# The causal mask of an attention head: from a TensorE product to an add inside VectorE's maximum pass

## The chip, the cores and the metric

The kernel runs on one core of a Trainium2 chip. A core has five engines with queues of their own: PE (TensorE: matrix products into PSUM; PEld is its weight load), DVE (VectorE), ACT (ScalarE), POOL (GpSimd) and SP, which here only issues DMAs. Each queue runs in the order in which the program was written out; engines wait for one another by semaphores. The metric is the device time of one execution in microseconds (us), lower is better.

## The reference

One decoder layer on 512 tokens of width 1024, in float32: a layer norm; an input projection; a gated linear attention branch in four heads; a latent attention branch in eight heads (MLA); gates, an output projection and a layer norm; a squared-ReLU MLP with hidden width 4096 and a last layer norm. The change is in the MLA heads, whose core is:

```
scale = MLA_QK ** -0.5                                  # MLA_QK = 192
for blk in range(seq // Q_BLOCK):                       # 4 blocks of 128 queries
    q0, q1 = blk * Q_BLOCK, (blk + 1) * Q_BLOCK
    s = (einsum('bhqd,bhkd->bhqk', q_nope[:, :, q0:q1], k_nope[:, :, :q1])
         + einsum('bhqr,bkr->bhqk', q_rope[:, :, q0:q1], k_rope[:, :q1])) * scale
    mask = (q0 + arange(Q_BLOCK))[:, None] >= arange(q1)[None, :]
    p = softmax(where(mask, s, -inf), axis=-1)
    outs.append(einsum('bhqk,bhkv->bhqv', p, v[:, :, :q1]))
```

So a block of 128 queries sees 128, 256, 384 or 512 keys, and only its last 128 columns need a mask: a triangle.

## The kernel before

Nearly every matrix product is made from split operands: a float32 array is rounded to a high part on ACT and its remainder, the low part, is made on DVE (`split`, and lines 180 and 181 in `pump` for the weights), and a product is then three products, high by high, high by low and low by high (lines 231 to 233, 264 to 266, 1134 to 1136). Weights come from HBM through a stream that is planned ahead: `pump` issues their DMAs on SP's queue (line 168) into three raw buffers, and splits them in turn.

Work that runs beside the big products is written as Python generators; `tick` steps each of them once after each weight block. The order on each engine is then set by the framework's scheduler, which reorders the whole program by its own estimate of time (`schedule_with_timeline_sim=True`), with a few `issue_after` gates. So an edit in one place can change the order of instructions in another place.

Start-up. Two of the four x tiles are loaded on SP's queue, then the first weights. DVE takes statistics of a tile in two halves (line 349), POOL takes the power of -0.5 (352), and the tile is normalised, on ACT for tile 0 (356, which waits for `nmr` of line 355) and on DVE for tile 1 (358). PE transposes them (367), ACT writes the high part `h` (370) and DVE the low part (374, 375). The first products (264 to 266) multiply them by the first weights, whose split is `xh` (180, ACT) and `xl` (181, DVE). Small constants are loaded on ACT's DMA queue: `cb` (line 395, a pack of gains, the 128x128 triangle `neg` and the frequencies `invf`), positions, level masks `lmi` and `wa`. `prep` turns them into what later stages need (413 to 421).

An MLA head (`mla_head`) goes through its four query blocks. For block i with n = 128(i+1) keys: five products into one PSUM bank (813 to 817); a sixth (818) adds the triangle by multiplying a bf16 identity with the bf16 triangle `negb` into the last 128 columns; DVE takes the negated row maximum `mx` from PSUM (820); ACT takes the exponential from PSUM with `mx` as bias, writes `Pm` to SBUF and sums the row (823); DVE inverts the sum and scales the row (824, 825). After the four blocks PE transposes the rows (837), they are split, and multiplied with the values. Heads are spawned in pairs, and run beside the projections of the next pair and of `w_o_gla` and `w_o_mla`. SBUF tiles come from pools: B has 22 buffers of 2 KB per partition, taken in turn.

The end. `ln2_stats` and `ln2` make the last layer norm, tile by tile, beside and behind the last products.

Of the kernel before, what the change touches and what calls it, by code (L numbers as in the profile page):

```python
# [10 lines left out]
F32 = mybir.dt.float32  # L11
F32R = mybir.dt.float32r
BF = mybir.dt.bfloat16
I32 = mybir.dt.int32
U8 = mybir.dt.uint8
AF = mybir.ActivationFunctionType
ALU = mybir.AluOpType
AX = mybir.AxisListType

P = 128  # L20
T = 512
# [27 lines left out]
PACK_B = 3 + 2 + NK + GH + 2 * NK + 2 * NK + P + 32  # L49
# [3 lines left out]
def tile_hybrid_block(ctx: ExitStack, tc: tile.TileContext, I, out, dbg=None):  # L53
    nc = tc.nc
    dbg = dbg or {}
    consts = ctx.enter_context(tc.tile_pool(name="consts", bufs=1))
# [8 lines left out]
    def nm(s):  # L65
        uid[0] += 1
        return f"{s}_{uid[0]}"
# [4 lines left out]
    def A(shape, dt=F32, n="a"):  # L72
        tag, bufs = ("C", 8) if n in TAG_C else (n, TAG_W[n]) if n in TAG_W else ("A", 24)
        return pa.tile(shape, dt, tag=tag, bufs=bufs, name=nm(n))

    def B(shape, dt=F32, n="b"):
        return pb.tile(shape, dt, tag="B", name=nm(n))

    def S(shape, dt=F32, n="s"):
        return sm.tile(shape, dt, tag=n, name=nm(n))  # L80
# [4 lines left out]
    def PX(shape=(P, T), dt=F32, n="px"):  # L85
        return px.tile(list(shape), dt, tag="px", name=nm(n))
# [4 lines left out]
    act = nc.scalar.activation  # L91
# [4 lines left out]
    mm = nc.tensor.matmul  # L96
# [7 lines left out]
    def split(src, hi, lo, scale=None):  # L104
        if scale is None:
            act(hi, src, AF.Copy)
            return vtt(lo, src, f(hi), op=ALU.subtract)
        else:
            act(hi, src, AF.Copy, scale=scale)
            return stt(lo, src, scale, f(hi), op0=ALU.mult, op1=ALU.subtract)  # L110
# [13 lines left out]
    ident = ca[:, 0:P]  # L124
# [2 lines left out]
    mhalf = consts.tile([P, 8], F32, name="mhalf")  # L127
    nc.vector.memset(mhalf, -0.5)
    identr = consts.tile([P, P], F32R, name="identr")
    identb = consts.tile([P, P], BF, name="identb")  # L130
    negb = consts.tile([P, P], BF, name="negb")


    stream = []
# [255 lines left out]


    act(identr, ident, AF.Copy)
    act(identb, ident, AF.Copy)
    cb = consts.tile([P, PACK_B], F32, name="cb")
    nc.scalar.dma_start(cb, I["c_pack_b"])
    cut = np.cumsum([0, 3, 2, NK, GH, 2 * NK, NK, NK, P, 32]).tolist()
    qag, kvg, glg, bga, bgt, ln1g, ln1b, neg, invf = [cb[:, cut[i]:cut[i + 1]] for i in range(9)]
    posi = consts.tile([P, NT], I32, name="posi")
    nc.scalar.dma_start(posi, I["positions"].rearrange("(t p) -> p t", p=P))
    lmask = consts.tile([P, len(LEVELS), 64], U8, name="lmask")  # L400
# [10 lines left out]
    def prep():  # L411
        with tc.issue_after(last_in.ins):
            vts(hbg, bgt, 0.5, None, op0=ALU.mult)
            nc.vector.tensor_copy(negb, neg)
            nc.vector.tensor_copy(lmask, lmi)
        posf = consts.tile([P, NT], F32, name="posf")
        with tc.issue_after(last_in.ins):
            nc.vector.tensor_copy(posf, posi)
        ang = B([P, NT, 32], F32, "ang")
        for tt in range(NT):  # L420
            vts(ang[:, tt, :], invf, posf[:, tt:tt + 1], None, op0=ALU.mult)
        yield
        angs = []
        for sh in (0.0, 0.25):
            kq = B([P, NT, 32], F32, "kq")
            vts(kq, ang, 1.0 / (2.0 * math.pi), sh, op0=ALU.mult, op1=ALU.add)
            vts(kq, kq, MAGIC, None, op0=ALU.add)
            vts(kq, kq, MAGIC, None, op0=ALU.subtract)
            r = B([P, NT, 32], F32, "rr")
            stt(r, kq, -TWO_PI_1, ang, op0=ALU.mult, op1=ALU.add)  # L430
            stt(r, kq, -TWO_PI_2, r, op0=ALU.mult, op1=ALU.add)
            stt(r, kq, -TWO_PI_3, r, op0=ALU.mult, op1=ALU.add)
            vts(r, r, sh * 2.0 * math.pi, PI_F, op0=ALU.add, op1=ALU.min)
            vts(r, r, -PI_F, None, op0=ALU.max)
            angs.append(r)
            yield
        act(sn2[:, :, 32:], angs[0], AF.Sin)
        act(cs2[:, :, :32], angs[1], AF.Sin)
        nc.vector.tensor_copy(cs2[:, :, 32:], cs2[:, :, :32])
        vts(sn2[:, :, :32], sn2[:, :, 32:], -1.0, None, op0=ALU.mult)  # L440
        yield
# [311 lines left out]
    scale = HQ ** -0.5  # L753
# [47 lines left out]
    def mla_head(h, hl, qn, kn, vt):  # L801
        for _ in range((0 if h == MH - 1 else STAG) * hl):
            yield
        KK, qs = KKs[0], QS[h]
        Ps = []
        P02 = B([P, T], F32, "P02")
        for i in range(NT):
            n = P * (i + 1)
            nn = max(n, 2 * P)
            c = slice(i * P, (i + 1) * P)  # L810
            p = PX()
            o = p[:, :nn]
            mm(o, qn[:, 0, c], kn[:, 0, :nn], start=True, stop=False)
            mm(o, qn[:, 0, c], kn[:, 1, :nn], start=False, stop=False)
            mm(o, qn[:, 1, c], kn[:, 0, :nn], start=False, stop=False)
            mm(o, qs[:, c], KK[:, 0, :nn], start=False, stop=False)
            mm(o, qs[:, c], KK[:, 1, :nn], start=False, stop=False)
            mm(p[:, c], identb, negb, start=False, stop=True)
            mx = S([P, 1], F32, "mx")
            nc.vector.tensor_reduce(mx, p[:, :n], axis=AX.X, op=ALU.max, negate=True)  # L820
            Pm = P02[:, :P] if i == 0 else P02[:, P:] if i == 2 else B([P, T], F32, "Pm")
            sme = S([P, 1], F32, "sme")
            act(Pm[:, :n], p[:, :n], AF.Exp, bias=mx, accum_out=sme)
            nc.vector.reciprocal(sme, sme)
            vts(Pm[:, :n], Pm[:, :n], sme, None, op0=ALU.mult)
            Ps.append(Pm)
            if i != 0:
                yield

        PT = [A([P, 2, T], F32R, "PT0"), A([P, 2, T], F32R, "PT1"), B([P, 2, 256], F32R, "PT2")]  # L830
        plan_t = ([(i, 0, i) for i in range(4)], [(i - 1, 1, i) for i in range(1, 4)] + [(3, 3, 3)],
                  [(i - 2, 2, i) for i in range(2, 4)])
        for b, (pl, pt) in enumerate(zip(plan_t, PT)):
            n = len(pl) * P
            p = PX()
            for cc, j, i in pl:
                nc.tensor.transpose(p[:, cc * P:(cc + 1) * P], Ps[i][:, j * P:(j + 1) * P], ident)  # L837
            split(p[:, :n], pt[:, 0, :], pt[:, 1, :])
            if b != 1:
                yield  # L840
        PT0, PT1, PT2 = PT
        while vt[NT - 1] is None:
            yield
        o = PX()
        for j in range(NT):
            c = slice(hl * P, (hl + 1) * P)
            vh, vl = vt[j][:, 0, c], vt[j][:, 1, c]
            if j == 0:
                ph, pl, od = PT0[:, 0, :], PT0[:, 1, :], o
            elif j == 1:  # L850
                ph, pl, od = PT1[:, 0, :384], PT1[:, 1, :384], o[:, 128:]
            elif j == 2:
                ph, pl, od = PT2[:, 0, :], PT2[:, 1, :], o[:, 256:]
            else:
                ph, pl, od = PT1[:, 0, 384:], PT1[:, 1, 384:], o[:, 384:]
            mm(od, vh, ph, start=j == 0, stop=False)
            mm(od, vh, pl, start=False, stop=False)
            mm(od, vl, ph, start=False, stop=j == NT - 1)
        yield
        om = A([P, 2, T], F32R, "omT")  # L860
        st["om"] = split(o, om[:, 0, :], om[:, 1, :])
        omT[h] = om
# [17 lines left out]
    for hf in range(2):  # L880
        if hf == 1:
            finish(t_ln1)
            t_prep = spawn(prep())
        for i in range(2):
            gemm_tm([PL["lat", i]], hT, half, ev_lat(i), tts=(2 * hf, 2 * hf + 1))
# [73 lines left out]
    t0, mv = mla_pair(0)  # L959
    mv()  # L960
    y_gla(1)
    t1, mv = mla_pair(1)
    mv(lambda: finish(*t0))
    t2, mv = mla_pair(2)
    mv(lambda: finish(*t1))
    t3, mv = mla_pair(3)
# [72 lines left out]
    LN2 = [None] * NT  # L1039

    def ln2_stats(tt, j, w=T, c0=0):
        if LN2[tt] is None:
            LN2[tt] = (S([P, 4 if tt == 3 else 2, 6], F32, f"bst{tt}"), S([P, 2], F32, "mv"))
        c = j * T + c0
        i = 2 * j + c0 // w if tt == 3 else j
        nc.vector.bn_stats(LN2[tt][0][:, i, :], res[tt][:, c:c + w])
# [69 lines left out]
    def win_f2(ci, hid):  # L1116
# [60 lines left out]
        for t in range(2):  # L1177
            with tc.issue_after(st["p6"].ins):
                ln2_stats(t, 0)
        for t in range(2):  # L1180
            o = tile_product((8, 9), t)
            vtt(res[t][:, T:], res[t][:, T:], o, op=ALU.add)
            ln2_stats(t, 1)
            ln2(t)
# [104 lines left out]
```

## Time and profile before

| | us |
|---|---|
| runs shown (3), median | 900.85 (900.52 to 900.86) |
| profiled execution, its own time | 900.46 |
| its span, first to last instruction | 898.7 |
| PE busy in the span | 878.0 |
| DVE busy | 570.2 |
| ACT busy | 432.7 |
| POOL busy | 172.8 |

The span is what the profile sees; 1.8 us of the execution's time lie around it. Where rows are shown, a timeline row is: start and length in us, engine, line, operation, output<-inputs, shape, count, and in brackets idle time before it and what ended that. A row by source line is: engine, operation, count, then the shortest, median and longest duration in ns, and the first and last start. A row by form gives busy us and mean ns after the bar. A row of windows is: the stretch, its length, then busy us (instructions) of PE, PEld, DVE, ACT and POOL, the granted PE clock, the share of DMA engines busy, and GB/s.

### The profile page before, as it was taken

How to read it: one execution, taken by the hardware profiler on the slowest of the kernel's cores; microseconds unless marked ns; L12 is line 12 of the kernel's file. 1: busy time of each engine (PE TensorE's matmuls, PEld its weight loads, DVE VectorE, ACT ScalarE, POOL GpSimd, SP SyncE). 2: the span in 40 equal slices, each digit the busy share in tenths (PEclk: the TensorE clock that was granted, in tenths of full speed). 3: DMA queues.
4: the chain of work that ended last, by engine and by line, in shares of the span. 5: the costliest groups of instructions: out<-in, count | busy, mean ns of one | idle time of the engine just before them, and what ended most of it. 6: DMA issues, size and time to landing. Idle time of an engine off the chain costs nothing.

```text
span 898.7 us, 11716 instructions
## 1 busy us (share of the span) xinstructions
PE 878.0 (98%) x4472; PEld 746.2 (83%) x4472; DVE 570.2 (63%) x927; ACT 432.7 (48%) x731; POOL 172.8 (19%) x201
## 2 busy tenths in 40 slices
PE   5999999999999999999999999999999999999995
PEld 5988888888888888888888888988888888888884
DVE  7835855575634243657765797998556656753687
ACT  5555443444444333435644424266457536644661
POOL 0003542443511010000000002103400520142022
PEclk9999999999999999999999999999999999999998
DMA  7413223212213332212206628004960991298075
GB/s 237 129 47 94 73 69 94 71 47 71 71 42 94 88 107 55 87 35 72 94 24 257 190 69 287 18 1 102 317 144 0 268 251 44 59 307 196 1 187 94
DMA packets 63048, 100.94 MB, mean 112 GB/s; under 512 B 7649, under 2 KB 31585, under 8 KB 62993
## 3 DMA queue, kind: packets, MB, share of 16 engines
q1 hardware_dynamic: 48256, 64.04, 23.2%
q0 software_dynamic: 12816, 32.51, 14.9%
q10 hardware_dynamic: 1920, 3.66, 1.2%
q8 instruction: 35, 0.57, 0.3%
q14 instruction: 21, 0.16, 0.1%
HBM read 82.36 MB, written 3.67 MB: 96 GB/s over the span
## 4 chain that ended last, share of the span: by engine, by line
PE 96%; ACT 1%; DVE 1%; POOL 1%; DMA 1%; issue 0%; POOLq 0%; SPq 0%; DVEq 0%; ACTq 0%
PE mm L231 16%; PE mm L233 15%; PE mm L232 15%; PE mm L264 6%; PE mm L266 6%; PE mm L265 6%; PE px L1134 3%; PE px L1135 3%; PE px L1136 3%; PE mm L1134 2%; PE mm L1135 2%; PE mm L1136 2%; PE px L680 2%; PE px L837 1%; PE px L266 1%; PE px L264 1%
## 5 line engine op out<-in xcount | busy, mean ns | idle before, releaser
L181 DVE TENSOR_TENSOR wlo<-wraw,whi 128x1024 fp32r<-128x1024 f32 (+1 forms) x104 | 117.7, 1133 | 164.4 <-ACT whi L180 157.1
L231 PE MATMUL mm<-h,whi 128*128 128x512 f32 x416 | 162.7, 392 | 0.4 <-ACT gt L924 0.4
L232 PE MATMUL mm<-h,whi 128*128 128x512 f32 x416 | 162.4, 390 | 0.0
L180 ACT ACTIVATE whi<-wraw 128x1024 fp32r<-128x1024 f32 (+1 forms) x104 | 100.3, 964 | 120.6 <-PE mm L232 69.8
L233 PE MATMUL mm<-h,wlo 128*128 128x512 f32 x416 | 154.9, 390 | 0.0
L1162 POOL DMA_DIRECT2D res<-ev x54 | 46.8, 978 | 240.1 <-ACT ev L1160 192.0
L231 PEld LDWEIGHTS mm<-h,whi 128*128 128x128 f32 x416 | 78.1, 188 | 16.4 <-ACT gt L924 0.6
L233 PEld LDWEIGHTS mm<-h,wlo 128*128 128x128 f32 x416 | 77.9, 188 | 16.3 <-DVE wlo L181 0.3
L232 PEld LDWEIGHTS mm<-h,whi 128*128 128x128 f32 x416 | 78.2, 188 | 15.6
L265 PE MATMUL mm<-wlo,h 128*128 128x512 f32 x128 | 50.3, 393 | 0.0
L266 PE MATMUL mm<-whi,h 128*128 128x512 f32 x128 | 50.2, 392 | 0.0
L264 PE MATMUL mm<-whi,h 128*128 128x512 f32 x128 | 49.7, 403 | 0.0
L1216 ACT ACTIVATE relu<-mm 128x512 f32<-128x512 f32 x32 | 18.8, 595 | 56.8 <-PE mm L233 56.8
L352 POOL TENSOR_TENSOR mv<-mv,mhalf 128x1 f32<-128x1 f32 x4 | 4.6, 1155 | 211.9 <-DVE mv L351 211.9
L619 POOL TENSOR_TENSOR rp<-rp 128x256 f32<-128x256 f32 x32 | 31.6, 986 | 60.3 <-ACT E L624 43.6
L626 DVE TENSOR_TENSOR M<-E,qk 128x512 f32<-128x512 f32 x32 | 26.9, 840 | 16.6 <-ACT E L624 16.6
L624 ACT ACTIVATE E<-rp 128x512 f32<-128x512 f32 x32 | 20.4, 638 | 27.7 <-POOL rp L620 27.7
L181 DVE TENSOR_TENSOR wlo<-wq,whi 128x1024 fp32r<-128x1024 f32 x15 | 18.3, 1223 | 19.7 <-ACT whi L180 19.7
L180 ACT ACTIVATE xh<-wraw 128x1024 fp32r<-128x1024 f32 (+1 forms) x20 | 18.7, 953 | 24.8 <-PE mm L266 15.8
L620 POOL TENSOR_TENSOR rp<-rp 128x256 f32<-128x256 f32 x32 | 28.5, 891 | 10.3 <-ACT q L649 8.1
L266 PEld LDWEIGHTS mm<-whi,h 128*128 128x128 f32 x128 | 24.1, 188 | 5.0
L265 PEld LDWEIGHTS mm<-wlo,h 128*128 128x128 f32 x128 | 24.1, 188 | 4.3
(374 smaller groups left out, 2237.7 us busy)
## 6 DMA issues: line engine op xcount, KB each, us to landing
wraw<-in_w_in_dram SPq DMA_DIRECT2D x40, 512.0 KB, 3.6
wraw<-in_w_ff_dram SPq DMA_DIRECT2D x32, 512.0 KB, 8.1
wq<-in_w_ff_dram POOLq DMA_DIRECT2D x32, 512.0 KB, 8.8
res<-ev POOLq DMA_DIRECT2D x54, 256.0 KB, 8.6
wraw<-in_w_o_gla_dram SPq DMA_DIRECT2D x8, 512.0 KB, 3.7
wraw<-in_w_o_mla_dram SPq DMA_DIRECT2D x8, 512.0 KB, 3.4
wraw<-in_w_out_dram SPq DMA_DIRECT2D x8, 512.0 KB, 4.4
wraw<-in_w_in_dram SPq DMA_DIRECT2D x8, 360.0 KB, 5.1
```

The source lines that it names most:

```text
L180: st["ins"] = act(hi[:, :nk, :n], raw[:, :nk, :n], AF.Copy)
L181: vtt(lo[:, :nk, :n], raw[:, :nk, :n], f(hi[:, :nk, :n]), op=ALU.subtract)
L231: mm(o, hi[:, c], xh, start=first, stop=False)
L232: mm(o, hi[:, c], xl, start=False, stop=False)
L233: mm(o, lo[:, c], xh, start=False, stop=last)
L264: mm(o, xh, hi[:, :n], start=opens, stop=False, skip_group_check=share)
L265: mm(o, xh, lo[:, :n], start=False, stop=False, skip_group_check=share)
L266: mm(o, xl, hi[:, :n], start=False, stop=last, skip_group_check=share)
L1134: mm(o, xh[:, c], hi[:, pp, cols], start=opens, stop=False, skip_group_check=True)
L1135: mm(o, xh[:, c], lo[:, pp, cols], start=False, stop=False, skip_group_check=True)
L1136: mm(o, xl[:, c], hi[:, pp, cols], start=False, stop=hf == 1 and pp == 1, skip_group_check=True)
L1162: nc.gpsimd.dma_start(res[tt + t][:, j * T:(j + 1) * T], e, accum_op=ALU.add)
```

## The change

The bf16 identity and triangle go, and with them the sixth product. A float32 mask `cmask` of 128x512 takes their place: zeros in its first 384 columns (written by POOL), the triangle in its last 128 (copied by DVE in `prep`). The maximum becomes one DVE instruction that adds the last n columns of `cmask` to the scores, multiplies by -1, writes that to `Pm` in SBUF, and folds the minimum of it into `mx`. In the built program each of these is two DVE instructions: the pass itself and a read of its accumulator into `mx` (128x1). The exponential then reads `Pm` from SBUF instead of the scores from PSUM, and writes in place, with scale -1.

To make room, the constant pack is loaded by two DMAs: `cb` keeps 49 columns, and the triangle and frequencies (160 columns) go to `cn`, a tile of pool B, whose DMA stands further back. The last layer norm's statistics tile moves to pool B.

```diff
-    identb = consts.tile([P, P], BF, name="identb")
-    negb = consts.tile([P, P], BF, name="negb")
+    cmask = consts.tile([P, T], F32, name="cmask")
...
-    act(identb, ident, AF.Copy)
-    cb = consts.tile([P, PACK_B], F32, name="cb")
-    nc.scalar.dma_start(cb, I["c_pack_b"])
+    nc.gpsimd.memset(cmask[:, :T - P], 0.0)
+    cb = consts.tile([P, PACK_B - P - 32], F32, name="cb")
+    nc.scalar.dma_start(cb, I["c_pack_b"][:, :PACK_B - P - 32])
+    cn = B([P, P + 32], F32, "cn")
+    nc.scalar.dma_start(cn, I["c_pack_b"][:, PACK_B - P - 32:])
...
-            nc.vector.tensor_copy(negb, neg)
+            nc.vector.tensor_copy(cmask[:, T - P:], neg)
...
-            mm(o, qs[:, c], KK[:, 1, :nn], start=False, stop=False)
-            mm(p[:, c], identb, negb, start=False, stop=True)
+            mm(o, qs[:, c], KK[:, 1, :nn], start=False, stop=True)
             mx = S([P, 1], F32, "mx")
-            nc.vector.tensor_reduce(mx, p[:, :n], axis=AX.X, op=ALU.max, negate=True)
             Pm = P02[:, :P] if i == 0 else P02[:, P:] if i == 2 else B([P, T], F32, "Pm")
+            nc.vector.tensor_tensor_reduce(Pm[:, :n], p[:, :n], cmask[:, T - n:], -1.0, 3.0e38,
+                                           op0=ALU.add, op1=ALU.min, accum_out=mx)
             sme = S([P, 1], F32, "sme")
-            act(Pm[:, :n], p[:, :n], AF.Exp, bias=mx, accum_out=sme)
+            act(Pm[:, :n], Pm[:, :n], AF.Exp, scale=-1.0, bias=mx, accum_out=sme)
...
-            LN2[tt] = (S([P, 4 if tt == 3 else 2, 6], F32, f"bst{tt}"), S([P, 2], F32, "mv"))
+            LN2[tt] = (B([P, 4 if tt == 3 else 2, 6], F32, "bst"), S([P, 2], F32, "mv"))
```

In the written-out order, 64 instructions leave PE (32 products with 32 weight loads), 32 come to DVE, one leaves ACT and one DMA joins its queue, one comes to POOL. SP's order is the same, and so is everything behind the first MLP block. In the start-up (about the first 40 us) and among the MLA heads the scheduler also put the remaining instructions in another order, and a few neighbours are swapped from there up to the first MLP block. In the start-up: on ACT the first `xh` split stands ahead of the normalisation of x tile 0 (before, behind it); on DVE both halves of tile 1's statistics stand ahead of `nmr` (before, one half); on ACT the fourth `xh` split stands after two evacuations `h` instead of after six `h` and two `lnt`; on DVE the statistics of tiles 2 and 3 both stand ahead of the split `xl` of the fifth weight block (before, those of tile 2 alone), and the copy into `cmask` stands ahead of the sixth.

More of the change, by code (lines that the diff above doesn't have):

```diff
@@ L392, in tile_hybrid_block @@
     act(identr, ident, AF.Copy)
-    act(identb, ident, AF.Copy)
-    cb = consts.tile([P, PACK_B], F32, name="cb")
-    nc.scalar.dma_start(cb, I["c_pack_b"])
+    nc.gpsimd.memset(cmask[:, :T - P], 0.0)
[3 more added lines that the diff above has]
+    nc.scalar.dma_start(cn, I["c_pack_b"][:, PACK_B - P - 32:])
     cut = np.cumsum([0, 3, 2, NK, GH, 2 * NK, NK, NK, P, 32]).tolist()
-    qag, kvg, glg, bga, bgt, ln1g, ln1b, neg, invf = [cb[:, cut[i]:cut[i + 1]] for i in range(9)]
+    qag, kvg, glg, bga, bgt, ln1g, ln1b = [cb[:, cut[i]:cut[i + 1]] for i in range(7)]
+    neg, invf = cn[:, :P], cn[:, P:]
     posi = consts.tile([P, NT], I32, name="posi")
```

## The prediction

> **What bounds the kernel now.** I read the page first, then the stretch of the MLA heads and a stretch of the start-up in the view of windows.
>
> ```profile
> span 898.7 us, 11716 instructions
> PE 878.0 (98%) x4472; PEld 746.2 (83%) x4472; DVE 570.2 (63%) x927; ACT 432.7 (48%) x731; POOL 172.8 (19%) x201
> PE 96%; ACT 1%; DVE 1%; POOL 1%; DMA 1%; issue 0%; POOLq 0%; SPq 0%; DVEq 0%; ACTq 0%
> ```
>
> PE is busy for 98% of the span and carries 96% of the chain that ended last: time taken off PE's queue is time gained, and a wait put on PE is time lost, almost anywhere.
>
> ```profile
> core 0: us, PE busy (x) PEld busy (x) DVE busy (x) ACT busy (x) POOL busy (x), PEclk, DMA share, GB/s
> 15.00:20.00 5.00, 5.00 (x31) 4.84 (x30) 4.91 (x14) 3.95 (x7) 0.00 (x0) 1.00 0.99 326
> 363.00:470.00 107.00, 107.00 (x622) 91.30 (x621) 71.04 (x170) 53.16 (x133) 0.00 (x0) 1.00 0.19 56
> ```
>
> Among the heads PE is never idle and DVE has 36 of 107 us free. In the start-up stretch DVE is as full as PE (4.91 of 5): there DVE's order matters.
>
> **The products removed.** The rows of line 818, then PE's queue around the first and the last of the 32:
>
> ```profile
> L818 PEld LDWEIGHTS <-identb x32: 94/96/99, 364.6 to 468.1; 128*128 128x128 bf16 x32
> L818 PE MATMUL px<-negb,identb x32: 220/230/233, 364.6 to 468.2; 128*128 128x128 bf16 x32
> ```
>
> ```profile
> 364.45 0.28 PE L817 MATMUL px<-KK,QS 128*128 128x256 f32 x1
> 364.57 0.23 PE L818 MATMUL px<-negb,identb 128*128 128x128 bf16 x1
> 364.61 0.36 PE L814 MATMUL px<-qn,qn 128*128 128x256 f32 x1
> 364.82 0.28 PE L815 MATMUL px<-qn,qn 128*128 128x256 f32 x1
> ...
> 467.92 0.39 PE L817 MATMUL px<-KK,QS 128*128 128x512 f32 x1
> 468.15 0.23 PE L818 MATMUL px<-negb,identb 128*128 128x128 bf16 x1
> 468.19 0.47 PE L231 MATMUL mm<-omT,whi 128*128 128x512 f32 x1
> 468.51 0.39 PE L232 MATMUL mm<-omT,whi 128*128 128x512 f32 x1
> ```
>
> Durations overlap, so the price is the distance of starts. Without a mask product a 256-column product takes 0.12 us from start to start (364.45 to 364.57), a 512-column one 0.23. From the mask product's start to the second product behind it are 0.25 and 0.36 us, which hold one such product: 0.13 us for each mask product, most of it in the product behind it. 32 x 0.13 is 4.2; I take 4.1, since beside a few small transposes it may be less. All of it lies on PE in a full stretch.
>
> The Trainium skill would make it less: "TensorE: Matmul & The Clock Gate", section "Back-to-back issue gap", gives 56 ns for an isolated 128-column product and about 81 ns for one with its weight load in a stream; by it the saving would be 1.8 or 2.6 us. Both are below what the starts in these rows show, 0.13; the row decides, and the rule stands as a rival.
>
> **The maximum pass.** It still reads the scores from PSUM, now beside a float32 operand in SBUF, and writes n columns instead of one. Rows by form, in the stretch of the heads:
>
> ```profile
> L820 DVE TENSOR_REDUCE mx<-px 128x1 f32<-128x512 f32 x8 | 5.5, 688 | 2.6 <-PE px L818 2.4
> L820 DVE TENSOR_REDUCE mx<-px 128x1 f32<-128x128 f32 x8 | 2.3, 286 | 3.3 <-PE px L818 3.3
> L107 DVE TENSOR_TENSOR PT<-px,PT 128x512 fp32r<-128x512 f32 x12 | 7.9, 684 | 4.1 <-ACT PT L106 4.1
> L824 DVE RECIPROCAL sme<-sme 128x1 f32<-128x1 f32 x32 | 5.0, 158 | 4.9 <-ACT Pm L823 3.2 <-ACT P L823 1.3
> ```
>
> The nearest row, a two-operand pass from PSUM over 512 columns, takes 684 ns against the maximum's 688: no change. The accumulator's read is shown nowhere; the nearest DVE row of 128x1 is 158 ns, so 32 x 0.16 = 5 us of DVE, 76 of 107 busy. `mx`, and all behind it, comes 0.16 us later, less the 0.13 that the scores are ready earlier. The cover is the projection products between the heads' own: I charge 0.1 us for one wait of PE, 0 to 0.5. The lower bound of pass and read is no change. Reading SBUF, the exponential no longer holds the PSUM bank, which comes free earlier; PE's waits for a bank are none in the heads, so that gains nothing. `act(identb)`, the cast of the triangle (now a copy), POOL's clear (POOL is idle before 6.5 us) and the statistics tile at the end (four of 22 buffers of pool B, long free) I cost at nothing: they lie beside x's first DMA, or beside PE.
>
> **The start-up, where the order moves.** The rows, by engine:
>
> ```profile
> 7.79 1.24 ACT L356 ACTIVATE x<-x,nmr,mvin 128x1024 f32<-128x1024 f32 x1 [2.64 <-DVE nmr L355]
> 8.94 2.18 ACT L180 ACTIVATE xh<-wraw 128x720 fp32r<-128x720 f32 x3
> 17.23 0.35 ACTq L402 DMA_DIRECT2D lmi<-in_c_lmask_dram  x1
> 17.62 0.44 ACTq L406 DMA_DIRECT2D wa<-in_w_gla_a_dram  x1
> ```
>
> ```profile
> 7.67 0.69 DVE L349 BATCH_NORM_STATS2 bst<-x 128x6 f32<-128x512 f32 x1
> 16.01 1.29 DVE L349 BATCH_NORM_STATS2 bst<-x 128x6 f32<-128x512 f32 x2
> 18.31 0.54 DVE L374 TENSOR_SCALAR lnt<-px,ca 128x256 f32<-128x256 f32 x1
> 18.77 0.42 DVE L375 TENSOR_TENSOR h<-lnt,h 128x256 fp32r<-128x256 f32 x1
> 19.22 0.86 DVE L181 TENSOR_TENSOR xl<-wraw,xh 128x720 fp32r<-128x720 f32 x1
> 20.32 1.28 DVE L349 BATCH_NORM_STATS2 bst<-x 128x6 f32<-128x512 f32 x2
> ```
>
> ```profile
> 9.09 1.12 PE L367 MATMUL px<-ca,x 128*128 128x128 f32 x4 [9.09 <-ACT x L356]
> 13.40 0.89 PE L367 MATMUL px<-ca,x 128*128 128x128 f32 x4 [0.36 <-DVE lnt L374]
> 20.51 0.49 PE L265 MATMUL mm<-xl,h 128*128 128x360 f32 x2
> ```
>
> ```profile
> wraw<-in_w_in_dram SPq DMA_DIRECT2D x1, 360.0 KB, 6.2
> posi<-in_positions_dram ACTq DMA_DIRECT2D x1, 2.0 KB, 7.1
> ...
> cb<-in_c_pack_b_dram ACTq DMA_DIRECT2D x1, 104.5 KB, 4.3
> ...
> lmi<-in_c_lmask_dram ACTq DMA_DIRECT2D x1, 224.0 KB, 3.4
> ```
>
> I walked the new order through: each instruction starts when its engine is free and its inputs are there, with these durations.
>
> (a) The first weight DMA is issued at 2.1 and lands 6.2 later, at 8.3. ACT now splits it first (2.18/3 = 0.73 us), so tile 0 is normalised from about 9.05, not 7.79 (`nmr`, now behind the second statistics, at 7.67 + 0.69, is in time). PE's first transpose moves from 9.09 to about 10.35. Part is won back: before, PE waited 0.36 at 13.40 for low halves on DVE behind three `xl`; now two stand there. But the fourth split stands ahead of four evacuations, so later low halves are late. After both, PE is 0.8 behind at 20 us (0.6 if 80 KB fewer ahead of the first weights land them 0.2 sooner; 1.0 at most).
>
> (b) DVE comes to the statistics of tile 2 at about 18.1, not 16.01: 0.86 for the fourth `xl`, which now stands ahead of them, 0.54 for a `lnt` that does too, and 0.7 in which DVE has to wait for the fourth split. Then come both pairs (1.29 + 1.28), two short casts (0.15) and a low half (0.42), less 0.2 of overlap: at about 21.0 the fifth `xl` starts (19.22 before), and ends 0.86 later at 21.9. PE takes it where row 20.51 was. In the new order fewer products stand ahead of that place, so PE is there at about 20.5 although (a) holds it back: a wait of 1.4 us.
>
> (c) `cn` is a DMA behind ACT's last evacuation, at about 18.5; it pushes `lmi`, `wa` and the next `xh` split back by its issue, 0.4. DVE comes to the copy into `cmask` at about 22.6, with the sixth `xl`, tiles 2 and 3, and through them the next weight DMA on SP queued behind it. Landing after 3.4 (as `lmi`) to 4.3 us (as `cb`), at 21.9 to 22.8, it holds DVE 0 to 0.2 us. Tiles 2 and 3 are normalised some 2 us later than before: I charge 0.3 more for PE's waits until 33 us (from -0.4, since waits there now may go, to 0.9).
>
> Start-up: 0.8 + 1.4 + 0.3 = 2.5, from 1.6 to 3.3. PE stays full behind it, so nothing takes it back.
>
> **Sum.** -4.1 + 2.5 + 0.1 = -1.5 us. On the profiled execution: span 898.7 to 897.2. Its own time, 900.46, is 0.4 under the median of 900.85; from the median 899.3. With the ends (-4.1 + 1.6 = -2.5; -4.0 + 3.3 + 0.5 = -0.2) this case runs from 898.3 to 900.6.
>
> **The rivals.**
> 1. The start-up costs little (other DMA times, the walk too strict): -4.1 + 0.5 gives 897.2. For it: DMAs start earlier, as the first raw buffer is freed sooner. Against: (a) and (b) hang on no DMA but the first. Chance 0.18.
> 2. Slower: `cn` lands late and DVE stands at the copy. With the 7.1 us of `posi` it lands at 25.6, holds DVE 3 us, and PE with it: -1.5 + 3 = 902.4. Below a hold of 1.5 us it is no loss; slower by 0.2% needs 3.3. Against: `posi` is 4-byte pieces, `lmi` took 3.4. Chance 0.10.
> 3. The mask pass runs at half rate. From 688 and 286 ns a column costs 1.05 ns; a head has 128 + 256 + 384 + 512 = 1280, eight heads 10240: 10.7 us more of DVE, 87 of 107 busy with the read. DVE still fits on average, so PE waits in bursts, 1 to 2 us by my estimate: 900.8. Chance 0.08. The Trainium skill speaks for it: "Vector Engine (DVE) Microarchitecture Reference", section "Points that are easy to get wrong", says that a two-tensor pass with two non-bf16 SBUF sources halves its throughput, with no port left for the accumulator. Here one source lies in PSUM, so it may not bind; no row of before shows it.
> 4. The mask product costs PE only 56 to 81 ns: -2.2 + 2.6 gives 901.2. Against: the starts above. Chance 0.04.
>
> **How the numbers follow.** The likeliest case has 0.60, centred at 899.3. A measurement of this kernel can tell about 0.2%, 1.8 us: faster is below 899.05, slower above 902.65. Of the 0.60, 0.23 lie below 899.05; with rival 1 faster is 0.41. Slower: most of rival 2 and tails, 0.11. The rest, 0.48, is within 0.2%. The range, 897.0 to 901.3, takes in rival 1, rival 3 and a hold of 2 us at `cn`.
>
> **What would show it.** PE's instructions fall by 32 products and the stretch of the heads by about 4 us, with PE still full. DVE's rows: a pass near 690 ns at 512 columns and a read near 0.16 us. PE's first transpose at about 10.3; a PE wait of over 1 us on `xl` between 20 and 22; the first product of the k projection about 2.5 us later than before. Wrong if these waits are missing, if the pass takes over 1 us, or if the copy into `cmask` waits for `cn` by more than 0.5 us.

## The result, and the profile after

The changed kernel takes 898.34 us (median of 10 runs, 897.99 to 898.87) where the kernel before takes 900.68 beside it: a ratio of 0.9976, 95% interval 0.9967 to 0.9986. Two repeats gave 898.43 (0.9975, 0.9966 to 0.9984) and 898.32 (0.9979, 0.9970 to 0.9988). It is faster by 2.0 to 2.3 us. Forecast was 899.3, a gain of 1.5. The profiled execution took 898.36.

The page of the changed kernel, the lines that answer to the first fence of the prediction, and then its windows:

```profile
span 896.6 us, 11680 instructions
...
PE 874.2 (98%) x4440; PEld 746.3 (83%) x4440; DVE 569.8 (64%) x959; ACT 432.7 (48%) x730; POOL 173.0 (19%) x202
...
PE 95%; DVE 1%; DMA 1%; ACT 1%; POOL 1%; issue 0%; POOLq 0%; SPq 0%; DVEq 0%; ACTq 0%
```

```profile
core 0: us, PE busy (x) PEld busy (x) DVE busy (x) ACT busy (x) POOL busy (x), PEclk, DMA share, GB/s
15.00:20.00 5.00, 5.00 (x31) 4.98 (x30) 4.97 (x14) 5.00 (x11) 0.00 (x0) 1.00 0.91 315
20.00:25.00 5.00, 4.08 (x25) 3.78 (x24) 4.48 (x13) 0.61 (x1) 1.36 (x2) 1.00 0.38 86
363.00:470.00 107.00, 106.97 (x613) 93.98 (x612) 71.56 (x202) 54.03 (x134) 0.00 (x0) 1.00 0.20 61
```

PE has 32 products fewer and is still full among the heads. DVE is no busier there: 71.56 of 107 us, 71.04 before. In the start-up PE is idle for 0.92 us between 20 and 25. The rows of the pass, and ACT's of the exponential, by form in the heads:

```profile
L822 DVE CUSTOM_DVE_ANT_0 Pm<-px,cmask 128x512 f32<-128x512 f32 x8 | 5.5, 686 | 4.6 <-PE px L819 4.4
...
L822 DVE DVE_READ_ACCUMULATOR2_ANT mx<- 128x1 f32 x32 | 2.7, 84 | 0.0
L822 DVE CUSTOM_DVE_ANT_0 P<-px,cmask 128x128 f32<-128x128 f32 x8 | 2.3, 288 | 5.9 <-PE px L819 5.8
```

```profile
L825 ACT ACTIVATE Pm<-Pm,mx 128x512 f32<-128x512 f32 x8 | 5.8, 725 | 11.6 <-DVE mx L822 11.6
...
L825 ACT ACTIVATE P<-P,mx 128x128 f32<-128x128 f32 x8 | 3.2, 401 | 2.0 <-DVE mx L822 2.0
```

The pass takes 686 and 288 ns at 512 and 128 columns, the plain maximum took 688 and 286. The read of the accumulator takes 84 ns, not the 158 that stood in for it. The exponential, from SBUF now, is longer than it was from PSUM in the kernel before:

```profile
L823 ACT ACTIVATE Pm<-px,mx 128x512 f32<-128x512 f32 x8 | 5.5, 688 | 7.7 <-DVE mx L820 7.7
...
L823 ACT ACTIVATE P<-px,mx 128x128 f32<-128x128 f32 x8 | 2.9, 368 | 5.4 <-DVE mx L820 5.4
```

The start-up, ACT, DVE and PE of the changed kernel in order of time:

```profile
8.09 0.80 ACT L179 ACTIVATE xh<-wraw 128x720 fp32r<-128x720 f32 x1 [3.56 <-DMA wraw<-in_w_in_dram]
8.80 1.23 ACT L355 ACTIVATE x<-x,nmr,mvin 128x1024 f32<-128x1024 f32 x1
...
16.33 0.35 ACTq L396 DMA_DIRECT2D cn<-in_c_pack_b_dram  x1
```

```profile
17.66 1.28 DVE L348 BATCH_NORM_STATS2 bst<-x 128x6 f32<-128x512 f32 x2
...
19.33 1.28 DVE L348 BATCH_NORM_STATS2 bst<-x 128x6 f32<-128x512 f32 x2
20.52 0.90 DVE L180 TENSOR_TENSOR xl<-wraw,xh 128x720 fp32r<-128x720 f32 x1
...
22.07 0.23 DVE L416 COPY cmask<-cn 128x128 f32<-128x128 f32 x1
```

```profile
10.08 1.12 PE L366 MATMUL px<-ca,x 128*128 128x128 f32 x4 [10.08 <-ACT x L355]
...
20.07 0.49 PE L263 MATMUL mm<-xh,h 128*128 128x360 f32 x2
21.48 0.43 PE L264 MATMUL mm<-xl,h 128*128 128x360 f32 x1 [0.92 <-DVE xl L180]
```

The first transpose stands at 10.08 (9.09 before), behind the first split; the fifth `xl` starts at 20.52 (19.22 before), behind both pairs of statistics, and PE waits for it. The copy into `cmask` shows no wait.

To part the start-up from the rest, three rows of each trace are enough: the first transpose, the start of the first head product (the first of the two times in its row; the table has it to two places) and the last product. Those of the two kernels are in the fences, two of before and then two of the changed kernel; the table has them for the experiments too. The last column, the way from the first head product to the last product, is free of what the start-up does.

```profile
L813 PE MATMUL px<-qn,qn x4: 283/312/397, 363.2 to 366.8; 128*128 128x256 f32 x2, 128*128 128x384 f32 x1, 128*128 128x512 f32 x1
```

```profile
888.48 0.28 PE L1136 MATMUL px<-xh,a 128*128 128x256 f32 x1
```

```profile
L815 PE MATMUL px<-qn,qn x4: 283/311/387, 364.8 to 368.0; 128*128 128x256 f32 x2, 128*128 128x384 f32 x1, 128*128 128x512 f32 x1
```

```profile
886.30 0.28 PE L1138 MATMUL px<-xh,a 128*128 128x256 f32 x1
```

| trace | first transpose | first head product | last product | from head to end |
|---|---|---|---|---|
| before | 9.09 | 363.20 | 888.48 | 525.3 |
| changed | 10.08 | 364.79 | 886.30 | 521.5 |
| changed, repeats | 10.15, 10.70 | 364.92, 365.28 | 886.43, 886.80 | 521.5, 521.5 |
| changed, pack in one DMA (twice) | 9.41, 9.37 | 363.70, 363.84 | 885.27, 885.44 | 521.6, 521.6 |
| before, with the start-up's part alone | 10.26 | 364.88 | 890.07 | 525.2 |
| before, without the sixth product | 8.78 | 362.81 | 884.08 | 521.3 |
| changed, old head of the start-up | 9.79 | 364.71 | 886.23 | 521.5 |
| changed, one DMA, first split early | 10.85 | 364.75 | 886.33 | 521.6 |
| extra pass in all blocks | 9.97 | 364.70 | 891.84 | 527.1 |
| extra pass behind the row | 10.90 | 365.56 | 891.86 | 526.3 |
| extra pass, 128-column blocks alone | 10.19 | 365.16 | 886.64 | 521.5 |
| extra pass, 256-column blocks alone | 10.57 | 365.41 | 891.68 | 526.3 |

So the heads give 525.3 - 521.5 = 3.8, and the start-up takes 364.8 - 363.2 = 1.6 (1.6 to 2.1 over the three traces of the changed kernel; the first transpose, which hangs on the first DMAs, moves by 0.6 among them). Single traces of one order differ, too: the kernel without the sixth product keeps the start-up's order of before, and its heads begin 0.4 us earlier.

### The profile page after: what moved, and what is told of

Read it like the earlier page. It is cut to its first block, busy times and chain, and to the rows that moved or that the text cites. A ratio compares the mean times of both kernels' runs of the same rounds, so it can differ in the third digit from the quotient of the medians.

```text
span 896.6 us, 11680 instructions
## 1 busy us (share of the span) xinstructions
PE 874.2 (98%) x4440; PEld 746.3 (83%) x4440; DVE 569.8 (64%) x959; ACT 432.7 (48%) x730; POOL 173.0 (19%) x202
## 4 chain that ended last, share of the span: by engine, by line
PE 95%; DVE 1%; DMA 1%; ACT 1%; POOL 1%; issue 0%; POOLq 0%; SPq 0%; DVEq 0%; ACTq 0%
PE mm L230 16%; PE mm L232 16%; PE mm L231 15%; PE mm L263 6%; PE mm L265 6%; PE mm L264 6%; PE px L1136 3%; PE px L1138 3%; PE px L1137 3%; PE mm L1137 2%; PE mm L1138 2%; PE mm L1136 2%; PE px L682 2%; DMA wraw<-in_w_in_dram 1%; PE px L839 1%; PE px L263 1%
```

## The experiments

**The start-up given back.** The changed kernel with the pack in one DMA again. In the built program that puts PE's order in the start-up back to that of before, and ACT's and DVE's nearly.

```diff
-    cb = consts.tile([P, PACK_B - P - 32], F32, name="cb")
-    nc.scalar.dma_start(cb, I["c_pack_b"][:, :PACK_B - P - 32])
-    cn = B([P, P + 32], F32, "cn")
-    nc.scalar.dma_start(cn, I["c_pack_b"][:, PACK_B - P - 32:])
+    cb = consts.tile([P, PACK_B], F32, name="cb")
+    nc.scalar.dma_start(cb, I["c_pack_b"])
...
-    qag, kvg, glg, bga, bgt, ln1g, ln1b = [cb[:, cut[i]:cut[i + 1]] for i in range(7)]
-    neg, invf = cn[:, :P], cn[:, P:]
+    qag, kvg, glg, bga, bgt, ln1g, ln1b, neg, invf = [cb[:, cut[i]:cut[i + 1]] for i in range(9)]
```

> The changed kernel, but the constant pack is loaded whole by one DMA, as in the kernel before; mask, pass and exponential stay changed. Theory (two terms: the start-up's new order costs 1.6 us, the heads give 3.75): the scheduler puts the start-up back into the old order, the first transpose is back near 9.1 us, PE's wait on the fifth xl at 20 us goes, and the time is 900.7 - 3.75 = 896.9 (896.5 to 897.4), 1.4 to 1.6 below the changed kernel. Rival (the split of the pack costs nothing, and the heads' gain is 2.2 to 2.4 alone): 898.3 to 898.5, as the changed kernel. In the profile: the first product of the k projection within 0.3 us of the kernel before's by theory; 1.5 us later by the rival.

896.56 us, 0.9958 of before (0.9945 to 0.9970). Then again, beside the changed kernel on one chip:

> The kernel of the first run (pack in one DMA, mask in the pass) once more, beside the changed kernel on the same chip. Expected 896.6, and 1.5 to 1.9 below the changed kernel; if the first run's distance was chance, within 0.5 of it.

> The changed kernel on that same chip, to stand beside the other three of this set: 898.1 to 898.5.

896.59 (0.9960, 0.9947 to 0.9974) and 898.32: 1.73 less. Its rows at PE and DVE:

```profile
9.41 1.12 PE L366 MATMUL px<-ca,x 128*128 128x128 f32 x4 [9.41 <-ACT x L355]
```

```profile
19.65 0.86 DVE L180 TENSOR_TENSOR xl<-wraw,xh 128x720 fp32r<-128x720 f32 x1
...
20.76 1.28 DVE L348 BATCH_NORM_STATS2 bst<-x 128x6 f32<-128x512 f32 x2
```

The fifth `xl` is ahead of the second pair of statistics again, at 19.65, and the wait of 0.92 is gone from PE. The first head product comes 0.5 and 0.6 us later than in the trace of before, not within the 0.3 expected; as two traces of the old order differ by 0.4, that is not told from scatter. By the times the theory of two terms holds: the masked pass did not need the start-up's loss. This kernel beats both others, by about 3.7 and 1.7 us.

**The start-up alone.** The kernel before, its heads untouched, with only the pack in two DMAs (the first diff turned round) and the statistics tile in pool B.

> The kernel before with the heads as they were (bf16 identity, triangle and the sixth product kept), and only the other part of the change: the constant pack in two DMAs, and the last layer norm's statistics tile in pool B. Theory (two terms): first transpose near 10.1 us, the wait on the fifth xl back, all products of the heads 1.6 us later than in the kernel before, nothing taken back: 902.3 (901.9 to 902.7). Rival (the order of the start-up costs nothing by itself, what was seen in the changed kernel's trace comes from the mask's copy and clear): 900.7, no change. If the start-up costs what the prediction said, 2.5: 903.2.

901.64 (1.0016, 1.0008 to 1.0025): 1.4 slower. Neither the clear of the mask nor the copy into it is there (the cast into `negb` reads `cn` instead), and from head to end it keeps 525.2. Its start-up has the changed kernel's order on PE, ACT and DVE, and PE waits 0.76 on the fifth `xl`: the loss comes with the two DMAs and the order that they bring. 2.5 is excluded, no loss too.

**The products alone.** The mask is left out.

```diff
-            mm(o, qs[:, c], KK[:, 1, :nn], start=False, stop=False)
-            mm(p[:, c], identb, negb, start=False, stop=True)
+            mm(o, qs[:, c], KK[:, 1, :nn], start=False, stop=True)
```

> The kernel before without the sixth product: the mask is left out altogether, so its output is not the reference's; maximum and exponential read PSUM as before. It prices the 32 products alone. By the distance of starts (0.128 us each, 4.03 in all): 900.7 - 4.0 = 896.7 (896.4 to 897.0). By the Trainium skill, TensorE: Matmul & The Clock Gate, section Back-to-back issue gap (56 or 81 ns each): 898.9 or 898.1. Against the first run of this set it tells what the masked pass and the exponential from SBUF cost beside it: by theory 0.2 us (one wait of PE in the heads); if the pass or its read cost PE more, up to 1.

896.06, 4.16 under the 900.22 of before in that set: 4.16 / 32 = 0.13 us a product. From head to end the trace gives 525.3 - 521.3 = 4.0. The interval, 0.9940 to 0.9965, is a saving of 3.2 to 5.4 us; the rule of 56 or 81 ns, 1.8 or 2.6, falls here. The masked pass and the exponential from SBUF cost 0.2 to 0.3 by the last column; by medians 896.56 - 896.06 = 0.5, which the intervals, over 1 us to either side, do not tell from nothing.

**Steps (a) and (b) by themselves.** Two kernels. In the first, the changed kernel with the first split written behind the normalisation of tile 0:

```diff
...
         for tt in range(2):
-            ln_rows(xt[tt], xt[tt], mvin[:, tt, :], on_act=tt == 0)
+            n0 = ln_rows(xt[tt], xt[tt], mvin[:, tt, :], on_act=tt == 0)
+            if tt == 0:
+                st["gates"] = (n0,)
+                pump(-1)
...
-    pump(-1)
```

> The changed kernel with its two DMAs for the pack, but the first weight split written behind the normalisation of x tile 0 and gated on it: step (a) of the prediction undone. The scheduler then also puts the split of the fifth block's low part ahead of tile 3's statistics again, so step (b) goes too; what stays of the start-up is cn as a DMA of its own and the copy from it, step (c). Theory (the start-up's 1.6 us are the two moves a and b): first transpose near 9.1 to 9.4 us, no wait on the fifth xl, 1.3 to 1.8 below the changed kernel: 896.6. Rival (the loss hangs on the second DMA and on what is queued behind it): within 0.4 of the changed kernel.

898.18: no better than the changed kernel beside it (898.43). By its time this is the rival's branch, within 0.4, and the theory's 896.6 failed; the first transpose is at 9.79, not at 9.1 to 9.4. The wait on the fifth `xl` is gone, but PE now waits where it did not:

```profile
31.39 0.43 PE L263 MATMUL mm<-xh,h 128*128 128x360 f32 x1 [0.20 <-ACT h L369]
...
32.66 0.44 PE L366 MATMUL px<-ca,x 128*128 128x128 f32 x2 [0.34 <-DVE lnt L373]
```

```profile
29.57 2.57 DVE L180 TENSOR_TENSOR wlo<-wraw,whi 128x1024 fp32r<-128x1024 f32 x2 [2.09 <-ACT whi L179]
32.06 0.99 DVE L373 TENSOR_SCALAR lnt<-px,ca 128x256 f32<-128x256 f32 x2
```

DVE, in this order, makes two `wlo` (2.57 us) ahead of the `lnt` that PE needs at 32. So the one wait was exchanged for others, made by the scheduler for this edit. The run doesn't say what step (c) costs in the changed kernel, and it doesn't show the rival's cause, the second DMA, either. In the second, the kernel with one DMA, but tile 0's normalisation gated on the first split:

```diff
...
-            act(dst, src, AF.Identity, scale=mv[:, 1:2], bias=nmr)
+            with tc.issue_after(st["in0"].ins):
+                act(dst, src, AF.Identity, scale=mv[:, 1:2], bias=nmr)
```

(`st["in0"]` is the first split.)

> The kernel of the first set with the pack in one DMA, but the normalisation of x tile 0 gated on the first weight split: step (a) of the prediction alone. In the built order the fifth block's low part stands ahead of tile 3's statistics, so step (b) is absent. If the two steps add up, as the prediction's sum has it, this costs 0.7 (what the changed kernel's trace shows of (a) at 18 us) against that kernel, 897.3, with the first transpose at 10.1 and no wait on xl. If the later places of ACT's splits and of the low halves cost by themselves, up to 1.6: 898.2, as the changed kernel. If DVE's later work takes the delay back: 896.6.

898.04 where before takes 900.56 beside it: 2.5 less, and the kernel with one DMA is 3.7 below before in both of its sets. So this order costs 1.2 (1.5 by the bare medians, which are of different sets), without any wait on `xl`: nearer to the expectation's second branch than to its 0.7. The first transpose is at 10.85, not 10.1, which is 1.44 later than 9.41; 1.05 of that is left at the first head product (0.91 against the repeat). In the first trace of the changed kernel the split starts at 8.09, here at 8.87:

```profile
8.87 0.80 ACT L179 ACTIVATE xh<-wraw 128x720 fp32r<-128x720 f32 x1 [3.80 <-DMA wraw<-in_w_in_dram]
9.57 1.23 ACT L357 ACTIVATE x<-x,nmr,mvin 128x1024 f32<-128x1024 f32 x1
```

So (a), with what the scheduler moves along with it, costs 0.9 to 1.2 where the pack is whole. That the smaller pack lands the first weights sooner is not shown: in the eight traces of kernels with two DMAs and the split first, it starts at 7.98 to 8.91. What (b) adds is seen where the split starts as late as here. The third trace of the changed kernel (split at 8.71, first transpose at 10.70, next to this 10.85) waits 1.10 on the fifth `xl`, and has its first head product 0.5 later (365.28 to 364.75).

The changed kernel stood beside these two and one of the next part:

> The changed kernel itself, to stand beside the three others of this set on the same chip. 0.9976 of the kernel before was measured: 898.1 to 898.5 where before takes 900.2 to 900.7.

898.43, as expected.

**Had the pass been slower.** One more DVE pass for each block, ahead of the masked pass and into the same row:

```diff
+            nc.vector.tensor_tensor(Pm[:, :n], p[:, :n], cmask[:, T - n:], op=ALU.add)
             nc.vector.tensor_tensor_reduce(Pm[:, :n], p[:, :n], cmask[:, T - n:], -1.0, 3.0e38,
```

> The changed kernel with one more DVE pass for each block: scores plus mask, from PSUM to the same row tile in SBUF, which the pass behind it then writes again. It adds 1280 columns for each head, 10240 in all, about 10.9 us of DVE at 1.05 ns a column and a latency of 0.29 to 0.69 us for each block: what the changed pass at half rate would have cost. If DVE's idle time in the heads covers it: 898.3 to 898.8. If PE then waits in bursts, as rival 3 of the prediction said: 899.3 to 900.3. If every block's latency (32 times 0.5) reaches PE: over 905.

902.62 (1.0030, 1.0018 to 1.0041), 2.4 above the 900.22 of before in that set and 4.3 above the changed kernel's 898.34 (of another set): between the second branch and the third. Then the pass where nobody waits for its output:

```diff
...
             vts(Pm[:, :n], Pm[:, :n], sme, None, op0=ALU.mult)
+            nc.vector.tensor_tensor(scr[:, :n], Pm[:, :n], cmask[:, T - n:], op=ALU.add)
```

> The changed kernel with one more DVE pass for each block, as many columns as in the fourth run of the first set, but behind the scaling of the row, from the row and the mask in SBUF to a tile that nobody reads: no block's own chain waits for it, only what is queued behind it on DVE. With the extra pass inside the chain the loss against the changed kernel was 4.3 us. If DVE's time is what lacks: again 3 to 5, 901.5 to 903. If it is the latency of the chain from scores to transposed rows: 898.3 to 899.3. [...]

903.10, 4.7 above the changed kernel on the same chip (898.43). So it isn't the latency of a block's own chain. (With both sources in SBUF the extra pass took 689 ns at 512 columns, no longer than with one in PSUM.) That left DVE's time, or the order: with any new instruction the scheduler orders the heads anew. Two runs tell them apart, with the extra pass of the first kind under `if i in (0,):` and under `if i in (1,):`.

> The changed kernel with the extra DVE pass (scores plus mask into the row's tile) in the first block of each head alone: 8 passes of 0.29 us, 2.3 us of DVE, where all 32 (10.9 us) cost 4.3. In the built order only neighbours are swapped in the heads. If what costs is DVE's time, in proportion: +0.9, 899.3. If what costs is the order that the scheduler makes around the pass: 0 to 0.3, 898.4 to 898.7.

> The same extra pass in the second block alone: 8 passes of 0.42 us, 3.4 us of DVE. Here the scheduler also moves weight splits and whole groups of the heads on ACT and DVE, as with all 32. By DVE's time in proportion: +1.4, 899.8. By the order: most of the 4.3, +2 to +4, 900.4 to 902.4, with a PE wait of over 1 us near 447 to 452 us and DVE standing for a high half of a weight (whi) ahead of it.

898.20 (0.9977, 0.9968 to 0.9986) and 902.00 (1.0021, 1.0012 to 1.0031), beside 898.32 of the changed kernel. 2.3 us of DVE cost nothing, 3.4 us cost 3.7: nearly the price of all 10.9. So the price does not go by DVE's time; it goes with the order. The heads of the last kernel, first the windows (columns as above), then ACT, DVE and PE:

```profile
440.00:450.00 10.00, 9.81 (x68) 8.83 (x66) 7.06 (x25) 5.99 (x15) 0.00 (x0) 1.00 0.17 52
450.00:460.00 10.00, 8.45 (x36) 7.10 (x37) 6.12 (x15) 3.87 (x10) 0.00 (x0) 0.83 0.17 54
```

```profile
448.58 1.06 ACT L179 ACTIVATE whi<-wraw 128x1024 fp32r<-128x1024 f32 x1 [0.42 <-ACT Pm L827]
449.54 1.06 ACT L106 ACTIVATE PT<-px 128x512 fp32r<-128x512 f32 x2
```

```profile
449.67 1.23 DVE L180 TENSOR_TENSOR wlo<-wraw,whi 128x1024 fp32r<-128x1024 f32 x1 [0.92 <-ACT whi L179]
450.81 0.55 DVE L824 CUSTOM_DVE_ANT_0 P<-px,cmask 128x384 f32<-128x384 f32 x1
451.29 0.08 DVE L824 DVE_READ_ACCUMULATOR2_ANT mx<- 128x1 f32 x1
451.29 1.28 DVE L107 TENSOR_TENSOR PT<-px,PT 128x512 fp32r<-128x512 f32 x2
```

```profile
449.47 0.34 PE L819 MATMUL px<-KK,QS 128*128 128x384 f32 x1
451.51 0.47 PE L860 MATMUL px<-PT,mv 128*128 128x512 f32 x1 [1.70 <-DVE mx L824]
```

PE's wait of 1.70 us ends with DVE's mask pass over 384 columns and its read into `mx`. The product that waits (line 860) takes only the high half of `PT`, which ACT had made by 450.60, and it writes to `px`, a pool of four PSUM tiles. So what it lacks is, as far as the rows show, a tile that this pass still has to read: with the exponential on SBUF, the pass is the last reader of the scores. The next product, at 452.03, needs the low half of `PT`, which stands behind the pass. On DVE both stand behind a weight's low half `wlo`, for which DVE has itself stood idle for 0.92 us until ACT had made `whi`. DVE is not fuller than in the changed kernel, which in the same stretch has `PT` and the pass ahead of `wlo` on DVE, and `PT` ahead of `whi` on ACT:

```profile
440.00:450.00 10.00, 10.00 (x69) 9.32 (x68) 8.89 (x26) 7.27 (x16) 0.00 (x0) 1.00 0.17 54
450.00:460.00 10.00, 9.97 (x61) 8.56 (x60) 5.40 (x19) 3.53 (x9) 0.00 (x0) 1.00 0.17 52
```

```profile
445.54 1.09 ACT L106 ACTIVATE PT<-px 128x512 fp32r<-128x512 f32 x2 [0.40 <-PE px L839]
...
447.73 1.09 ACT L179 ACTIVATE whi<-wraw 128x1024 fp32r<-128x1024 f32 x1
```

```profile
446.17 1.29 DVE L107 TENSOR_TENSOR PT<-px,PT 128x512 fp32r<-128x512 f32 x2 [0.44 <-ACT PT L106]
...
448.57 0.55 DVE L822 CUSTOM_DVE_ANT_0 P<-px,cmask 128x384 f32<-128x384 f32 x1
...
449.38 1.22 DVE L180 TENSOR_TENSOR wlo<-wraw,whi 128x1024 fp32r<-128x1024 f32 x1
```

What all 32 passes would cost in the changed kernel's own order wasn't tried.

## Why the prediction was right, and where its numbers were off

The forecast's case came in: time won on PE by the products, less time lost in the start-up by the order. The gain of 1.5 was 0.5 to 0.8 too small, and the size of one term, the start-up, explains it.

- **The products, -4.1.** Right: 4.16 by medians, 4.0 by the trace. The distance of starts was the right way to price them; a duration of 230 ns would have given 7.4. The estimate by the Trainium skill ("TensorE: Matmul & The Clock Gate", section "Back-to-back issue gap") was 1.8 to 2.6. Here a 128-column bf16 product stood between float32 ones; why it costs more than the Trainium skill says was not tried.
- **The pass and its read, 0.1.** The pass costs what the maximum did; the read half of what was taken (84 to 158 ns). What the prediction left out: the exponential from SBUF takes 32 to 37 ns more in each block's chain. The whole came to 0.2 to 0.5, within the 0 to 0.5 given.
- **The start-up, 2.5 (1.6 to 3.3).** This is the term mis-sized: 1.4 alone on the kernel before, 1.6 between the traces, 1.7 against the kernel with one DMA, at the lower end or under it. The walk had the places right and, for this trace, each size too large. Counted product by product (the start of the k-th product in the one trace less that in the other), PE is 1.0 late at the first transpose and 0.7 just ahead of the wait: step (a), for which 0.8 was given. The first split started at 8.09, not 8.3, and the transpose came at 10.08, not 10.35; in the third trace they came at 8.71 and 10.70, and (a) is 0.95 there, so 0.8 is within the scatter. The pause on the fifth `xl` brings this to 1.8: step (b) is 1.1 (1.3 in the third trace), not 1.4, and the wait on `xl` that was to be over 1 us was 0.92 (0.92 and 1.10 in the repeats). The statistics began at 17.66 (18.1 forecast) and the fifth `xl` at 20.52 (21.0). From there to the heads 0.2 are won back: step (c) has the other sign, -0.2 for +0.3. `cn` was issued at 16.33, not 18.5, and DVE did not stand at the copy. So 0.7 + 1.1 - 0.2 = 1.6. That is the account of one pair of traces; no run has the steps one by one with everything else kept.
- **Rival 1** (start-up 0.5) is excluded by the run with the start-up alone, whose interval begins at 0.7 us. **Rival 2** (DVE stands at the copy) by the row at 22.07. **Rival 4** by the run without the mask.
- **Rival 3** (half rate) fell by its premise, 686 ns for 688. The rule behind it in the Trainium skill ("Vector Engine (DVE) Microarchitecture Reference", section "Points that are easy to get wrong") is for two sources in SBUF, and with one in PSUM it did not show. But its price, 1 to 2 us "in bursts", was too small as well: the doubled pass cost 4.3 and ended slower than before (902.6). By the runs with 8 extra passes that is the order which changes, more than DVE being full; for all 32 it was not parted.

## What to carry to other kernels

Price an instruction on a full engine by the distance of starts around it, and then look at what else the edit moves: here a constant pack loaded in two parts took 1.4 to 1.7 of the 3.8 us that the heads had won, and loading it whole gave a kernel faster than both. Where a scheduler orders the whole program, the price of an added instruction is not its time (2.3 us of DVE were free, 3.4 us cost 3.7): compare the orders on each engine before judging a cost, and try a variant that keeps the old one.

## What the runs showed that was not expected

A pause of PE can cost more than itself. After the wait of 1.70 us the granted clock, full in the stretch before, falls (the kernel with the extra pass in the 256-column blocks, windows of 1 us, columns as above):

```profile
451.00:452.00 1.00, 0.47 (x1) 0.19 (x1) 1.00 (x4) 1.00 (x4) 0.00 (x0) 1.00 0.04 12
452.00:453.00 1.00, 0.97 (x4) 0.88 (x5) 1.00 (x2) 0.45 (x2) 0.00 (x0) 0.92 0.87 254
453.00:454.00 1.00, 1.00 (x4) 0.71 (x4) 1.00 (x3) 0.00 (x0) 0.00 (x0) 0.50 0.67 258
...
455.00:456.00 1.00, 1.00 (x7) 1.00 (x5) 0.70 (x2) 0.19 (x1) 0.00 (x0) 0.50 0.00 0
456.00:457.00 1.00, 1.00 (x6) 0.87 (x5) 0.30 (x2) 0.63 (x2) 0.00 (x0) 0.88 0.00 0
457.00:458.00 1.00, 1.00 (x6) 0.82 (x5) 0.35 (x1) 0.00 (x0) 0.00 (x0) 1.00 0.00 0
```

It is at one half from about 452.8 to 456.2, which loses 0.08 + 3 x 0.5 + 0.12 = 1.7 us on top of the wait. The traces with the extra pass in all blocks (a wait of 2.11) and behind the row (1.70) show the same; the waits of 0.92 and 1.10 in the changed kernel's start-up did not do this (granted clock 1.00 from 20 to 25). The Trainium skill ("TensorE: Matmul & The Clock Gate", section "HAM oscillation — how this bites in real kernels") warns of gaps of PE over some 3.4 us; here gaps of 1.70 to 2.11 were followed by it. Not each execution pays: of the ten of this kernel three have a mean granted clock of 0.995 and take 902.74 to 903.49 (the profiled one is among them), seven have 0.997 and take 901.21 to 902.26. With the extra pass in all blocks three of seven pay, behind the row seven of eleven. By the medians of the others the three kernels are still 3.6, 4.1 and 3.1 us above the changed kernel, so the clock is the smaller part of what the order costs.

The exponential takes longer from SBUF than it did from PSUM: 401 and 725 ns at 128 and 512 columns against 368 and 688. It now also writes in place and has a scale of -1; which of the three makes the difference was not tried.
